# Low parts of split weights: an accumulating SBUF-to-SBUF DMA in place of a GpSimd subtraction, in the first two mixers

## The chip, the core and the metric

One core of a Trainium2 chip runs the whole program. Its engines run their own instruction streams in order: TensorE (PE; its weight loads are listed apart as PEld), VectorE (DVE), ScalarE (ACT), GpSimd (POOL) and SyncE (SP), which here only issues DMAs. The metric is the device time of one execution in microseconds.

## The reference

The reference is a stack of ten phases on a sequence of 512 tokens with 1024 features, all in float32. The first block has two layers; each is a mixer and a feed-forward block. The second block has two layers of a mixer, cross attention to 256 memory tokens, and a feed-forward block. The change touches the mixers of the first block:

```
h    = rmsnorm(x, g)
proj = h @ w_in          # 1024 x 4896: qa ka va | qd kd vd | beta, decay | z | two gates
y_attn = attention(rope(rmsnorm(qa)), rope(rmsnorm(ka)), va) @ w_o_attn
q, k, v = silu(depthwise_conv_5(qd | kd | vd)); q, k = l2norm(q), l2norm(k)
o    = gated_delta(q, k, v, beta, g) + flip(gated_delta(flipped))   # 8 chunks of 64 tokens, 8 heads
y_dn = rmsnorm(o) * silu(z) @ w_o_dn
x    = x + (sigmoid(gate0) * y_attn + sigmoid(gate1) * y_dn) @ w_out
```

In the gated delta rule each chunk needs the inverse of a unit triangular 64x64 matrix for each head and direction, and then a scan over the chunks.

## The kernel before

**Split products.** A float32 product is made of three matmuls in PE's fp32r format: both the weights and the activations are split into a high part (the value rounded to fp32r) and a low part (the value less the high part). `proj` (lines 480 to 491) does for each of a projection's chunks of 128 features: high weights by high activations (L487), high weights by low activations (L490), low weights by high activations (L491), all into one PSUM bank of 128x512.

**Weights.** The weights lie in HBM packed by groups of 256 output columns: row p of a group holds, for each of kc chunks of 128 input features, 256 columns. `fetch` (L459) loads a group with one DMA from SP into a `wraw` tile of a pool of two buffers. `wload` (L464) then cuts the group into pieces of four chunks by 128 columns (128x512 numbers): ACT casts a piece into `whi` (L474), and POOL subtracts, `wlo = wraw - whi` (L475 through the helper `tt`, L383). Both `whi` and `wlo` have four buffers, so a group of 8 chunks fills them once; a piece's cast waits until PE has used the piece four places before. The value weights of the cross attention are cut by pairs of chunks with all 256 columns (`rows=True`).

**A mixer** (`_mix`, L642) has 19 groups of `win` (`in_win`), one narrow group `wbd` of 32 columns, eight groups of 128 columns each of `woa` and `wod`, and four groups of `wout`. Its work is written as generators that are merged by hand with estimated costs: first the convolutions (`conv_tile`, L688 to L698: ACT scales, DVE adds four shifted taps at L697) and the norms (`l2`, with `rsqrt` L385 to L398 on small tiles); then `inside` (L820), which builds the chunk matrices with ACT, DVE and POOL (L843 to L853) and stores them to scratch tensors in HBM (`dnscr`, `scrK`, `scrN`, `scrT`), beside the projections of v and z; then `solve` (L1012), DVE's 30 steps of the triangular inverse on the tile N (loaded from `scrN` and `scrT`), beside the attention's projections; then the attention's core (L933), and the scan (L1180 to L1250) beside the `woa` projection; then the `wod` projection, the output projection `wout`, and the next phase's norm. The Tile framework allocates the buffers, places the semaphores, and orders each engine's stream by its own planner's costs, in the order of emission where nothing speaks against it.

SP's queue carries all weight fetches and all scratch stores and loads in one order. POOL's queue holds the subtracts, and in `inside` three to four 128x512 tensor operations for each pair of heads and direction.

Of the kernel before, what the change touches and what calls it, by code (L numbers as in the profile page):

```python
# [11 lines left out]
F32 = mybir.dt.float32  # L12
F32R = mybir.dt.float32r
I32 = mybir.dt.int32
AF = mybir.ActivationFunctionType
ALU = mybir.AluOpType
# [4 lines left out]
P = 128  # L21
S = 512
D = 1024
# [21 lines left out]
def _pack_cols(w, kc, cg):  # L45

    w = np.asarray(w)
    L, K, N = w.shape
    g = N // cg
    a = w.reshape(L, kc, P, g, cg).transpose(0, 3, 2, 1, 4)  # L50
    return np.ascontiguousarray(a).reshape(L, g, P, kc * cg)


def _cols(v):
# [115 lines left out]
EV_HEADS = ((1, 0), (0, 0), (1, 1), (0, 1), (1, 2), (0, 2), (0, 3), (1, 3))  # L170
# [35 lines left out]
def host_arrays(inputs):  # L206
    g = lambda k: np.asarray(inputs[k])
    A = {}
    A["x"] = np.ascontiguousarray(g("x")[0].T).reshape(8, P, S)
    A["mem"] = _pack_cols(np.asarray(g("mem_2")).transpose(0, 2, 1), 8, NMEM)[0, 0]  # L210
    A["vec"] = _vec_layout(inputs)[1]
    A["cst"] = CST_ARR
    A["rope"] = np.ascontiguousarray(_rope_tables())
    A["rett"] = _ret_tables()
    A["hgm"] = _hg_masks()
    A["dsat"] = _dsa_tables()
    A["relb"] = np.concatenate([g("rel_bias_2"), np.ones((1, 8), np.float32)], axis=0)
    w = g("w_in")
    qa, ka, va = w[..., :512], w[..., 512:640], w[..., 640:768]
    qd, kd, vd = w[..., 768:1280], w[..., 1280:1792], w[..., 1792:2304]  # L220
    bd, z, gate = w[..., 2304:2336], w[..., 2336:2848], w[..., 2848:]

    by_head = lambda a: a.reshape(2, -1, 2, 2, 2, 64).transpose(0, 1, 2, 4, 3, 5).reshape(2, -1, 512)
    z = by_head(z)
    qa = qa.reshape(2, D, 4, P)[..., PERM_A].reshape(2, D, 512)
    ka = ka[..., PERM_A]
    A["win"] = _pack_cols(np.concatenate([kd, qd, vd, qa, ka, va, z, gate], axis=-1), 8, 256)
    A["wbd"] = _pack_cols(bd, 8, 32)
    A["woa"] = _pack_cols(g("w_o_attn"), 4, 128)
    A["wod"] = _pack_cols(by_head(g("w_o_dn").transpose(0, 2, 1)).transpose(0, 2, 1), 4, 128)  # L230
    A["wout"] = _pack_cols(g("w_out"), 8, 256)
    A["wup"] = _pack_cols(g("w_up"), 8, 256)
    for nm, key in (("wdn", "w_down"), ("fdn", "ffn_w_out_2")):
        w = g(key)
        A[nm] = np.concatenate([_pack_cols(w[:, :1024], 8, 256), _pack_cols(w[:, 1024:2048], 8, 256)], axis=1)
        A[nm + "c"] = _pack_cols(w[:, 2048:], 6, 256)

    ev, eo = g("ev_w_in_2").reshape(1, D, 8, 4, P), g("ev_w_out_2").reshape(1, 2, 4, P, D)
    ev = [ev[:, :, 5]] + [ev[:, :, (slice(0, 4), [4, 6, 7])[i == 0], h] for i, h in EV_HEADS]
    A["evin"] = _pack_cols(np.concatenate(ev, axis=2).reshape(1, D, 4096), 8, 256)  # L240
    A["evout"] = _pack_cols(np.concatenate([eo[:, 1 - i, h] for i, h in EV_HEADS], axis=1), 8, 256)

    od = g("od_w_in_2").reshape(1, D, 3, 8, P).transpose(0, 1, 3, 2, 4).reshape(1, D, 3072)
    A["odin"] = _pack_cols(od, 8, 256)
    A["odout"] = _pack_cols(g("od_w_out_2"), 8, 256)
    A["xaq"] = _pack_cols(g("xa_w_q_2"), 8, 256)
    A["xakv"] = _pack_cols(g("xa_w_kv_2"), 8, 256)
    A["xao"] = _pack_cols(g("xa_w_o_2"), 8, 256)
    A["fup"] = _pack_cols(g("ffn_w_in_2"), 8, 256)
    return A  # L250


# [53 lines left out]
class Prog:  # L306
    def __init__(self, ctx, tc, A, out, first):
        self.ctx, self.tc, self.nc, self.A, self.out = ctx, tc, tc.nc, A, out
        nc = self.nc
        pool = lambda name, bufs=1, **kw: ctx.enter_context(tc.tile_pool(name=name, bufs=bufs, **kw))  # L310
        self.cp = pool("cp")
        self.xp = pool("xp")
        self.wr = pool("wr", 2)
        self.whl = pool("whl", 4)
        self.actp = pool("actp", 8)
        self.nrm = pool("nrm")
        self.psb_ = pool("psb", 2, space=PSUM)
        self.dr = pool("dr", 1, space=DRAM)
        self.ph = None

        self.vect = self.cp.tile([P, NVEC], F32, name="vect")
        self.cst = self.cp.tile([P, NCST], F32, name="cstt")
        self.x = [self.xt() for m in range(8)]
        self.xsrc = A["x"]
        nc.scalar.dma_start(out=self.vect, in_=A["vec"])
        nc.scalar.dma_start(out=self.cst, in_=A["cst"])

        self.first = []
        for m in range(8):
            nc.sync.dma_start(out=self.x[m], in_=A["x"][m])  # L330
            if m == 1:
                self.first = [self.fetch(s, 8, n) for s, n in first]
        self.ident = self.c("ident")
        self.ones = self.c("ones")
# [121 lines left out]
        return ps  # L456


    def fetch(self, src, kc, cg):  # L459
        raw = self.wr.tile([P, kc, cg], F32, name="wraw", tag="wraw")  # L460
        self.nc.sync.dma_start(out=raw, in_=src.rearrange("p (k c) -> p k c", k=kc))
        return raw

    def wload(self, src, kc, cg, rows=False):  # L464


        nc = self.nc
        raw = self.first.pop(0) if self.first else self.fetch(src, kc, cg)
        step, width = (2, cg) if rows else (4, min(P, cg))

        def piece(k, o):
            part = raw[:, k:min(k + step, kc), o:o + width]
            hi, lo = (self.whl.tile(list(part.shape), F32R, name=n, tag=n) for n in ("whi", "wlo"))
            nc.scalar.copy(hi, part)  # L474
            self.tt(lo, part, hi.bitcast(F32), ALU.subtract, "gpsimd")  # L475
            return k, hi, lo

        return [[piece(k, o) for k in range(0, kc, step)] for o in range(0, cg, width)]

    def proj(self, ps, w, acts, n=S, behind=None):  # L480

# [48 lines left out]
    def out_proj(self, wsrc, acts, nxt, k0=0, scale=None, final=True, behind=None):  # L530
        nc = self.nc
        kc = len(acts)
        for g in range(4):
            ws = self.wload(wsrc[g][:, k0 * 256:(k0 + kc) * 256], kc, 256)
            for j in range(2):
                m = 2 * g + j
                ps = self.psb()
                self.proj(ps, ws[j], acts, behind=behind)
                if scale is None:
                    self.tt(self.x[m], ps, self.x[m], ALU.add)  # L540
                else:
                    nc.vector.scalar_tensor_tensor(self.x[m], ps, scale, self.x[m], ALU.mult, ALU.add)
                if final:
                    self.x_done(m, nxt)
# [92 lines left out]

    def mix(self, l, nm, nxt):
        with self.phase("mix") as mp:
            self._mix(l, nm, nxt, mp)  # L640

    def _mix(self, l, nm, nxt, mp):  # L642
        nc, tc = self.nc, self.tc
# [976 lines left out]
    def _cross(self, l, nm, nxt, xp):  # L1620
        nc, gs = self.nc, self.gs
        wkv, wq = self.A["xakv"][l], self.A["xaq"][l]
# [26 lines left out]
        for k in range(8):  # L1649
            a = gs("mact", 8, (P, 2, M), F32R)  # L1650
            g = self.vec(f"xm{l}", k)
            hi = nc.scalar.activation(a[:, 0], mem[:, k], AF.Copy, scale=g)
            lo = nc.vector.scalar_tensor_tensor(a[:, 1], mem[:, k], g, a[:, 0].bitcast(F32), ALU.mult, ALU.subtract)
# [18 lines left out]
        for h in range(4):  # L1672
            ws = self.wload(wkv[h], 8, 256)
# [9 lines left out]
            for x in ks:  # L1683
                self.tt(x, x, ps, ALU.mult)
                kn.append(gs("kn", 4, (P, 2, M), F32R))
                self.split(kn[-1], x)
            ws = self.wload(wkv[4 + h], 8, 256, rows=True)
            vt = [gs("vt", 4, (P, 2, M), F32R) for _ in range(2)]
            pv = [self.psb() for _ in range(2)]
            for t in range(2):  # L1690
                tok = slice(t * P, (t + 1) * P)
                o = pv[t][:, :M]
                for k, hi, lo in ws[0]:
                    for i in range(2):
                        nc.tensor.matmul(o, ma[k + i][:, 0, tok], hi[:, i], start=k + i == 0, stop=False)
                        nc.tensor.matmul(o, ma[k + i][:, 0, tok], lo[:, i], start=False, stop=False)
                        nc.tensor.matmul(o, ma[k + i][:, 1, tok], hi[:, i], start=False, stop=k + i == 7)
                v = gs("kx", 3, (P, M))
                nc.scalar.activation(v, o, AF.Copy, scale=mr.rc[:, t])
                self.split(vt[t], v, "gpsimd")  # L1700
# [3 lines left out]
            for q2 in range(2):  # L1704
                ps = self.psf()
                for t in range(2):
                    tk, o = slice((2 * q2 + t) * P, (2 * q2 + t) * P + P), ps[:, t * M:t * M + M]
                    for i in range(2):
                        a, b = qs[i], kn[i]
# [9 lines left out]
                for t in range(2):  # L1719
                    p = pr[:, t * M:t * M + M]  # L1720
# [3 lines left out]
                for t in range(2):  # L1724
                    p = pr[:, t * M:t * M + M]
# [64 lines left out]
```

## Time and profile before

| | |
|---|---|
| median of three timed runs | 3455.85 us (3452.78 to 3457.21) |
| profiled execution | 3445.89 us |
| span from its first to its last instruction | 3444.1 us |
| mean granted TensorE clock | 0.979 of 2.4 GHz |
| busy: PE, PEld, DVE, ACT, POOL | 94%, 77%, 59%, 43%, 52% |
| first mixer, by its weight fetches and last matmuls | about 0 to 538 us |
| second mixer | about 886 to 1422 us |

The profiled execution and the timed runs are different executions; a sum made from the profile stands against 3445.89 us. Busy shares over the whole span mix phases that are bound by PE with phases that are not, so the stretches have to be looked at one by one.

### The profile page before, as it was taken

What the parts mean: (1) busy time and instruction counts of PE and PEld (TensorE: products, weight loads), DVE (VectorE), ACT (ScalarE), POOL (GpSimd) and SP (SyncE); (2) the same over time, 40 slices, a digit from 0 to 9 for tenths busy, and PEclk for the clock granted to TensorE, in tenths of its full rate; (3) what the DMA queues carried; (4) which work ended last, traced back from release to release, by engine and by line L of the source; (5) the groups of instructions that cost most, each with busy time, mean ns of one, the idle gap of its engine ahead of it and who ended that gap; (6) DMA issues with size and microseconds to landing.
All of it is one profiled execution on the core that took longest, in us unless ns stands there. A gap on an engine that the chain in (4) does not pass through costs nothing. (4 is left out here: it accounts for less than half of the span.)

```text
span 3444.1 us, 46891 instructions
## 1 busy us (share of the span) xinstructions
PE 3227.7 (94%) x17342; PEld 2655.6 (77%) x17342; DVE 2030.8 (59%) x3571; ACT 1483.2 (43%) x2766; POOL 1806.1 (52%) x1493
## 2 busy tenths in 40 slices
PE   8888899999987889999999898999999998999999
PEld 6666778888766667788877776878888887888887
DVE  8988555554698866464466676553223786653222
ACT  4526534343553553443353325443334444544332
POOL 4653365444565434654456556565556335555554
PEclk9999999999998999999999998999999999999999
DMA  4532542222354234222232113223223212222222
GB/s 148 160 89 62 119 127 98 98 89 92 121 158 124 73 81 133 100 99 92 98 112 86 62 47 103 85 99 121 94 98 107 78 67 101 88 87 98 98 97 87
DMA packets 135869, 342.53 MB, mean 99 GB/s; under 512 B 43056, under 2 KB 80304, under 8 KB 106969
## 3 DMA queue, kind: packets, MB, share of 16 engines
q1 hardware_dynamic: 134208, 336.04, 30.5%
q10 hardware_dynamic: 1432, 3.49, 0.4%
q8 instruction: 138, 2.26, 0.3%
q14 instruction: 91, 0.74, 0.1%
HBM read 312.15 MB, written 29.97 MB: 99 GB/s over the span
## 5 line engine op out<-in xcount | busy, mean ns | idle before, releaser
L383 POOL TENSOR_TENSOR wlo<-wraw,whi 128x512 fp32r<-128x512 f32 (+2 forms) x1044 | 1369.1, 1316 | 1397.9 <-ACT whi L474 1359.6
L474 ACT CAST whi<-wraw 128x512 fp32r<-128x512 f32 (+2 forms) x1044 | 631.5, 608 | 1129.5 <-PE psb L490 835.2
L487 PE MATMUL psb<-act,whi 128*128 128x512 f32 x1888 | 758.8, 402 | 59.6 <-DVE x L383 19.6
L491 PE MATMUL psb<-act,wlo 128*128 128x512 f32 x1888 | 751.5, 399 | 3.2 <-POOL wlo L383 3.0
L490 PE MATMUL psb<-act,whi 128*128 128x512 f32 x1888 | 752.6, 399 | 0.8 <-DVE act L277 0.6
L487 PEld LDWEIGHTS psb<-act,whi 128*128 128x128 f32 x1888 | 363.5, 193 | 140.0 <-issue 43.4
L491 PEld LDWEIGHTS psb<-act,wlo 128*128 128x128 f32 x1888 | 362.2, 192 | 81.1 <-POOL wlo L383 5.6
L490 PEld LDWEIGHTS psb<-act,whi 128*128 128x128 f32 x1888 | 363.4, 192 | 75.0 <-DVE act L277 2.3
L383 DVE TENSOR_TENSOR x<-psb,x 128x512 f32<-128x512 f32 x168 | 115.2, 689 | 377.0 <-PE psb L491 376.6
L487 PE MATMUL ps<-act,whi 128*128 128x512 f32 (+1 forms) x720 | 280.7, 390 | 3.4 <-ACT rB L303 3.4
L491 PE MATMUL ps<-act,wlo 128*128 128x512 f32 (+1 forms) x720 | 280.2, 389 | 0.0
L490 PE MATMUL ps<-act,whi 128*128 128x512 f32 (+1 forms) x720 | 280.2, 389 | 0.0
L487 PE MATMUL psb<-mid,whi 128*128 128x512 f32 x704 | 276.7, 394 | 1.0 <-DVE x L383 1.0
L491 PE MATMUL psb<-mid,wlo 128*128 128x512 f32 x704 | 276.2, 392 | 0.0
L490 PE MATMUL psb<-mid,whi 128*128 128x512 f32 x704 | 273.6, 389 | 0.0
L487 PEld LDWEIGHTS ps<-act,whi 128*128 128x128 f32 (+1 forms) x720 | 133.9, 186 | 33.7 <-ACT rB L303 4.6
L491 PEld LDWEIGHTS ps<-act,wlo 128*128 128x128 f32 (+1 forms) x720 | 133.9, 186 | 29.4
L490 PEld LDWEIGHTS ps<-act,whi 128*128 128x128 f32 (+1 forms) x720 | 133.9, 186 | 29.1
L491 PEld LDWEIGHTS psb<-mid,wlo 128*128 128x128 f32 x704 | 132.1, 188 | 30.5
L487 PEld LDWEIGHTS psb<-mid,whi 128*128 128x128 f32 x704 | 132.3, 188 | 29.3 <-DVE x L383 1.5
L490 PEld LDWEIGHTS psb<-mid,whi 128*128 128x128 f32 x704 | 132.1, 188 | 29.5
L383 DVE TENSOR_TENSOR cv<-ps,cv 128x512 f32<-128x512 f32 (+1 forms) x60 | 41.5, 692 | 175.9 <-PE ps L491 106.5
(437 smaller groups left out, 5712.3 us busy)
## 6 DMA issues: line engine op xcount, KB each, us to landing
wraw<-in_wup SPq DMA_DIRECT2D x44, 1024.0 KB, 4.8
wraw<-in_fup SPq DMA_DIRECT2D x44, 1024.0 KB, 4.8
wraw<-in_win SPq DMA_DIRECT2D x38, 1024.0 KB, 5.0
wraw<-in_wdn SPq DMA_DIRECT2D x16, 1024.0 KB, 4.8
wraw<-in_evin SPq DMA_DIRECT2D x16, 1024.0 KB, 4.8
wraw<-in_xakv SPq DMA_DIRECT2D x16, 1024.0 KB, 4.9
wraw<-in_fdn SPq DMA_DIRECT2D x16, 1024.0 KB, 4.8
wraw<-in_odin SPq DMA_DIRECT2D x12, 1024.0 KB, 4.9
```

The costliest lines, as they stand in the source:

```text
L383: getattr(self.nc, eng).tensor_tensor(out, a, b, op)
L474: nc.scalar.copy(hi, part)
L487: mm = nc.tensor.matmul(ps, hi[:, i], acts[k][:, 0, :n], start=k == 0, stop=False)
L490: nc.tensor.matmul(ps, hi[:, i], acts[k][:, 1, :n], start=False, stop=False)
L491: nc.tensor.matmul(ps, lo[:, i], acts[k][:, 0, :n], start=False, stop=k == kc - 1)
```

## The change

In the two first mixers a piece's low part is made in another way. ACT casts the high part as before; ACT then writes the negative of the high part into `wlo`; and a DMA from POOL's queue adds the piece of `wraw` to it, SBUF to SBUF (`accum_op=ALU.add`). In all other phases POOL subtracts as before. For all groups of 256 columns the packing in HBM becomes two halves of 128 columns, each with its chunks behind one another, so that a piece is one run of 2 KB in each row of `wraw`; `out_proj` now names the chunks that it wants (`k0`, `n`) in place of a slice. The value weights of the cross attention keep the old packing (`wrows`).

```diff
+def _pack_tiles(w, kc):
+    a = _pack_cols(w, kc, 256)
+    L, g = a.shape[:2]
+    return np.ascontiguousarray(a.reshape(L, g, P, kc, 2, P).transpose(0, 1, 2, 4, 3, 5)).reshape(L, g, P, kc * 256)
...
-    A["win"] = _pack_cols(np.concatenate([kd, qd, vd, qa, ka, va, z, gate], axis=-1), 8, 256)
+    A["win"] = _pack_tiles(np.concatenate([kd, qd, vd, qa, ka, va, z, gate], axis=-1), 8)
...
-    def fetch(self, src, kc, cg):
-        raw = self.wr.tile([P, kc, cg], F32, name="wraw", tag="wraw")
-        self.nc.sync.dma_start(out=raw, in_=src.rearrange("p (k c) -> p k c", k=kc))
-        return raw
+    def fetch(self, src, kc, cg, k0=0, n=None):
+        n, w = n or kc, min(P, cg)
+        raw = self.wr.tile([P, cg // w, n, w], F32, name="wraw", tag="wraw")
+        self.nc.sync.dma_start(out=raw, in_=src.rearrange("p (j k c) -> p j k c", k=kc, c=w)[:, :, k0:k0 + n])
+        return raw
+
+    def parts(self, part):
+        nc = self.nc
+        hi, lo = (self.whl.tile(list(part.shape), F32R, name=n, tag=n) for n in ("whi", "wlo"))
+        nc.scalar.copy(hi, part)
+        if self.lo_dma:
+            nc.scalar.activation(lo, hi.bitcast(F32), AF.Copy, scale=-1.0)
+            nc.gpsimd.dma_start(out=lo, in_=part, accum_op=ALU.add)
+        else:
+            self.tt(lo, part, hi.bitcast(F32), ALU.subtract, "gpsimd")
+        return hi, lo
+
+    def wload(self, src, kc, cg=256, k0=0, n=None):
+        raw = self.first.pop(0) if self.first else self.fetch(src, kc, cg, k0, n)
+        n = raw.shape[2]
+        return [[(k, *self.parts(raw[:, j, k:min(k + 4, n)])) for k in range(0, n, 4)] for j in range(raw.shape[1])]
...
-            ws = self.wload(wsrc[g][:, k0 * 256:(k0 + kc) * 256], kc, 256)
+            ws = self.wload(wsrc[g], wsrc[g].shape[-1] // 256, k0=k0, n=kc)
...
     def mix(self, l, nm, nxt):
         with self.phase("mix") as mp:
+            self.lo_dma = True
             self._mix(l, nm, nxt, mp)
+            self.lo_dma = False
```

## Rows read from the trace of the kernel before

**Rows 1.** The page, part 1: busy us, share of the span, instructions.
```profile
PE 3227.7 (94%) x17342; PEld 2655.6 (77%) x17342; DVE 2030.8 (59%) x3571; ACT 1483.2 (43%) x2766; POOL 1806.1 (52%) x1493
```

**Rows 2.** Stretches: length, each engine's busy us (instructions), clock, DMA share, GB/s.
```profile
560.00:900.00 340.00, 339.68 (x1493) 280.01 (x1492) 179.58 (x200) 136.93 (x226) 172.31 (x133) 1.00 0.28 98
...
45.00:220.00 175.00, 146.61 (x718) 119.61 (x717) 154.77 (x223) 85.42 (x161) 96.90 (x67) 0.92 0.51 139
...
sum 495.00, PE 409.42 PEld 331.03 DVE 439.83 ACT 241.14 POOL 262.08; mean PE 102.36 PEld 82.76 DVE 109.96 ACT 60.28 POOL 65.52
```

**Rows 3.** Timeline from 80 us: start, us, engine, line, operation, names, count.
```profile
80.61 0.18 DVE L383 TENSOR_TENSOR rsq<-rc 128x32 f32<-128x32 f32 x1
...
81.27 0.60 ACT L474 CAST whi<-wraw 128x512 fp32r<-128x512 f32 x1
81.31 0.68 DVE L383 TENSOR_TENSOR x<-x,cstt 128x512 f32<-128x512 f32 x1
...
81.95 2.99 POOL L383 TENSOR_TENSOR wlo<-wraw,whi 128x512 fp32r<-128x512 f32 x2 [2.52 <-ACT whi L474]
82.02 1.78 DVE L697 SCALAR_TENSOR_TENSOR kq<-pad,vect,kq 128x512 f32<-128x512 f32 x1
...
84.92 0.74 DVE L697 SCALAR_TENSOR_TENSOR kq<-pad,vect,kq 128x512 f32<-128x512 f32 x1
```

**Rows 4.** DVE's groups by form, 45 to 220 us: busy, mean ns, idle before.
```profile
L697 DVE SCALAR_TENSOR_TENSOR kq<-pad,vect,kq 128x512 f32<-128x512 f32 x22 | 21.0, 954 | 2.0 <-ACT kq L695 1.8
L697 DVE SCALAR_TENSOR_TENSOR cv<-pad,vect,cv 128x512 f32<-128x512 f32 x16 | 16.6, 1041 | 1.0 <-ACT cv L695 0.8
...
L383 DVE TENSOR_TENSOR x<-x,kkqq 128x512 f32<-128x512 f32 x8 | 12.3, 1556 | 0.0
...
L397 DVE SCALAR_TENSOR_TENSOR rsq<-rsq 128x32 f32<-128x32 f32 x6 | 3.1, 509 | 0.1
```

**Rows 5.** Waits: DVE's of 45 to 220, PE's of 45 to 300: us, times, longest.
```profile
DVE x L383 <- PE psb L491: 6.0, 1, 6.0
DVE ntmp L383 <- DMA N<-scrT: 5.9, 1, 5.9
DVE kq L697 <- ACT kq L695: 1.8, 3, 0.9
...
PE psb L487 <- DVE x L383: 9.7, 4, 3.8
...
PE psb L491 <- POOL wlo L383: 1.1, 1, 1.1
```

**Rows 6.** The stretches of rows 2, instructions that touch wlo: PE, PEld, POOL.
```profile
45.00:220.00 175.00, 65.81 (x161) 32.12 (x161) 55.93 (x38) 0.92 0.51 139
...
sum 495.00, PE 165.64 PEld 80.92 POOL 148.17; mean PE 41.41 PEld 20.23 POOL 37.04
```

**Rows 7.** DMA issues of 256 KB: queue, count, KB each, median us to landing.
```profile
dnscr<-s SPq DMA_DIRECT2D x32, 256.0 KB, 3.4
...
ti<-N SPq DMA_DIRECT2D x16, 256.0 KB, 5.1
...
xsp<-x SPq DMA_DIRECT2D x8, 256.0 KB, 2.0
```

**Rows 8.** Timeline of SP around the wod weights.
```profile
479.52 0.33 SPq L461 DMA_DIRECT2D wraw<-in_wod  x1
...
482.46 0.33 SPq L461 DMA_DIRECT2D wraw<-in_wout  x1
...
485.40 0.33 SPq L461 DMA_DIRECT2D wraw<-in_wout  x1
```

**Rows 9.** Timeline of PE, the first and the last of nine matmuls.
```profile
21.01 0.40 PE L487 MATMUL psb<-act,whi 128*128 128x512 f32 x1
...
22.88 0.39 PE L491 MATMUL psb<-act,wlo 128*128 128x512 f32 x1
```

**Rows 10.** Timeline of ACT in the same place, with its idle time.
```profile
482.66 0.62 ACT L474 CAST whi<-wraw 128x512 fp32r<-128x512 f32 x1 [1.26 <-DMA wraw<-in_wod]
```

More of the change, by code (lines that the diff above doesn't have):

```diff
@@ L230, in host_arrays @@
     A["wod"] = _pack_cols(by_head(g("w_o_dn").transpose(0, 2, 1)).transpose(0, 2, 1), 4, 128)
-    A["wout"] = _pack_cols(g("w_out"), 8, 256)
-    A["wup"] = _pack_cols(g("w_up"), 8, 256)
+    A["wout"] = _pack_tiles(g("w_out"), 8)
+    A["wup"] = _pack_tiles(g("w_up"), 8)
     for nm, key in (("wdn", "w_down"), ("fdn", "ffn_w_out_2")):
         w = g(key)
-        A[nm] = np.concatenate([_pack_cols(w[:, :1024], 8, 256), _pack_cols(w[:, 1024:2048], 8, 256)], axis=1)
-        A[nm + "c"] = _pack_cols(w[:, 2048:], 6, 256)
+        A[nm] = np.concatenate([_pack_tiles(w[:, :1024], 8), _pack_tiles(w[:, 1024:2048], 8)], axis=1)
+        A[nm + "c"] = _pack_tiles(w[:, 2048:], 6)
     ev, eo = g("ev_w_in_2").reshape(1, D, 8, 4, P), g("ev_w_out_2").reshape(1, 2, 4, P, D)
     ev = [ev[:, :, 5]] + [ev[:, :, (slice(0, 4), [4, 6, 7])[i == 0], h] for i, h in EV_HEADS]
-    A["evin"] = _pack_cols(np.concatenate(ev, axis=2).reshape(1, D, 4096), 8, 256)
-    A["evout"] = _pack_cols(np.concatenate([eo[:, 1 - i, h] for i, h in EV_HEADS], axis=1), 8, 256)
+    A["evin"] = _pack_tiles(np.concatenate(ev, axis=2).reshape(1, D, 4096), 8)
+    A["evout"] = _pack_tiles(np.concatenate([eo[:, 1 - i, h] for i, h in EV_HEADS], axis=1), 8)
     od = g("od_w_in_2").reshape(1, D, 3, 8, P).transpose(0, 1, 3, 2, 4).reshape(1, D, 3072)
[L244 to L249, printed above, removed]
+    A["odin"] = _pack_tiles(od, 8)
+    A["odout"] = _pack_tiles(g("od_w_out_2"), 8)
+    A["xaq"] = _pack_tiles(g("xa_w_q_2"), 8)
+    w = g("xa_w_kv_2")
+    A["xakv"] = np.concatenate([_pack_tiles(w[..., :1024], 8), _pack_cols(w[..., 1024:], 8, 256)], axis=1)
+    A["xao"] = _pack_tiles(g("xa_w_o_2"), 8)
+    A["fup"] = _pack_tiles(g("ffn_w_in_2"), 8)
     return A
@@ L456, in spread, with wrows @@
         return ps
-    def fetch(self, src, kc, cg):
-        raw = self.wr.tile([P, kc, cg], F32, name="wraw", tag="wraw")
-        self.nc.sync.dma_start(out=raw, in_=src.rearrange("p (k c) -> p k c", k=kc))
-        return raw
[L464 to L478, printed above, removed]
+    def fetch(self, src, kc, cg, k0=0, n=None):
[17 more added lines that the diff above has]
+        return [[(k, *self.parts(raw[:, j, k:min(k + 4, n)])) for k in range(0, n, 4)] for j in range(raw.shape[1])]
+    def wrows(self, src, kc):
+        raw = self.wr.tile([P, kc, 256], F32, name="wraw", tag="wraw")
+        self.nc.sync.dma_start(out=raw, in_=src.rearrange("p (k c) -> p k c", k=kc))
+        return [(k, *self.parts(raw[:, k:k + 2])) for k in range(0, kc, 2)]
     def proj(self, ps, w, acts, n=S, behind=None):
@@ L639, in mix @@
         with self.phase("mix") as mp:
+            self.lo_dma = True
             self._mix(l, nm, nxt, mp)
+            self.lo_dma = False
     def _mix(self, l, nm, nxt, mp):
@@ L1686, in _cross @@
                 self.split(kn[-1], x)
-            ws = self.wload(wkv[4 + h], 8, 256, rows=True)
+            ws = self.wrows(wkv[4 + h], 8)
             vt = [gs("vt", 4, (P, 2, M), F32R) for _ in range(2)]
@@ L1692, in _cross @@
                 o = pv[t][:, :M]
-                for k, hi, lo in ws[0]:
+                for k, hi, lo in ws:
                     for i in range(2):
```

## The prediction, made before the change was run

> **What bounds the kernel now.** I read the page's busy line first: TensorE (PE) is busy 94% of the span, so at most 6% can be won anywhere [rows 1]. Then busy time by stretch, to see where PE's idle time is. In the first feed-forward block PE has no gap at all: 339.7 of 340 us; a change there can only lose. In the two mixers it is different. The four stretches 45 to 300 us and 960 to 1200 us are 495 us long, and there VectorE (DVE) is the fullest engine with 439.8 us (89%), PE has 409.4 (83%), ScalarE (ACT) 241.1 and GpSimd (POOL) 262.1 [rows 2]. The 86 us that PE lacks there are most of what the mixers can give back.
>
> Next the timeline, for why DVE is full. A multiply-add of line 697 on 128x512 takes 0.74 us when POOL is quiet; the one that starts at 82.02, while POOL runs two weight subtracts, takes 1.78. A 128x512 tensor-tensor with two SBUF operands takes 0.68, a 128x32 step 0.18 [rows 3]. The groups of DVE's instructions by form tell how often this happens: the means lie far above those free durations [rows 4]. DVE's instructions with two operands in SBUF are stretched while POOL works.
>
> Last the waits, for who waits on whom. In 45 to 220 us DVE's idle time ends with PE once (6.0 us) and with the load of N once (5.9); the longest total on ACT is 1.8. PE for its part waits mostly for DVE to empty its banks (9.7 in one group), and only 1.1 us, once, for a low part [rows 5]. So in these stretches the order of cause is POOL, then DVE, then PE.
>
> **The change, part by part.** By the code a mixer has 19 column groups of four pieces, two pieces of wbd, eight each of woa and wod, and four groups of wout: 76 + 2 + 16 + 16 = 110 pieces, 220 in both. A piece is 128x512 numbers of whi and of wlo.
>
> *POOL's subtract is removed.* In 45 to 220 us it is 55.9 of POOL's 96.9 us, in the four stretches 148.2 of 262.1 [rows 2, 6]. What DVE gets back: from the groups, 22 x (954 - 740) ns = 4.7 us, 16 x (1041 - 740) = 4.8, 8 x (1556 - 680) = 7.0, and 6 x (509 - 180) = 2.0 for line 397, whose two companions in the same chain I count alike, 5.9 in all [rows 3, 4]. That is 22.4 us seen in a few groups. Bounds: below, only the subtract's share of POOL's time, 58%, gives 13; above, each subtract costs DVE its own length, 55.9. I take 25, near what is seen, since smaller groups add and POOL's other work takes away: 0.45 us of DVE per us of subtract. Over the four stretches that is 0.45 x 148.2 = 66 us, and DVE falls from 440 to 374, under PE's 409. PE becomes the fullest. Now the fullest engine reaches 89%; if PE then reaches 90%, the 495 us become 454: **41 us gained**. Bounds: 0 where dependences hold the stretch, 64 at 95% (431 us). I take 41, since it only asks that PE be served as well as DVE is now. The stretches outside are PE's already and I give them nothing.
>
> *ACT's negative is added.* It is a pass like the cast, 0.60 us [rows 3]: 220 x 0.60 = 132 us, of which 100 pieces, 60 us, fall in the four stretches; ACT goes to 301 of 454 us, 66%. Behind it wait ACT's tanh, copies and scalings, and DVE behind those. As DVE hardly waits for ACT there [rows 5], it is mostly covered by ACT's idle time; **5 us**, bounds 0 and 60.
>
> *The accumulating DMA is added.* The trace has no DMA that is issued from POOL and none that adds. Its 256 KB land 2.0 to 5.1 us after the issue in plain transfers [rows 7]. I take 4.5 from the end of the negative to the landing, near the slow end, since it reads two sources and shares the engines. The issue itself costs POOL at least SP's 0.33 us [rows 8] and, by the nearest POOL row, about what the subtract cost (1.5 us each, [rows 3]); between these POOL is no fuller than now, so nothing is charged. The Trainium skill prices it lower: its page "DMA: Bandwidth & Descriptors", section "Anatomy of one DMA — SWDGE (gpsimd) path", gives about 2.0 us plus bytes over 436 GB/s, 2.6 us for a piece as an estimate; the lateness below would shrink to some 4 us and the profile to about 3416 us.
>
> *How late is the low part?* whi and wlo have four buffers. Nine matmuls start in 2.1 us, 0.234 us apart [rows 9], so a piece of twelve lasts PE 2.8 us and a freed buffer is wanted again 8.4 us later. Now cast and subtract take 0.6 + 1.5 of it; then 0.6 + 0.6 + 4.5 = 5.7. That leaves 2.7 us, so in a steady row nothing waits. It fails in three places. (1) At the start there is no lead: 0.6 + 4.5 - 1.5 = 3.6 us later, **3 us** charged once. (2) wod: its pieces come one by one through the two raw buffers, and a buffer's next fetch waits until the low part has been made. SP issues these fetches 2.94 us apart now [rows 8], and ACT already waits for their data [rows 10]. The cycle grows by 3.6 us for two buffers, 1.8 a piece; for the four of eight that aren't fetched beforehand 7.2, less 2.7 of lead, about 5 a mixer, **10 us**. (3) Scattered places with a short lead, such as the one wait above [rows 5]: **4 us** for both. SP's own queue stands behind the raw buffer too (the stores of dnscr, scrN and scrT); with the 5.9 us wait for N in view I charge **2 us**.
>
> *The packing by 128 columns* moves no work: the fetches bring the same bytes in one piece. Only the half fetches of three later output projections become two runs per row; they are issued a group ahead and PE works meanwhile, so nothing; with that cover gone an SP issue of 0.33 us [rows 8] more for each of some three dozen, 12 us.
>
> Sum: 41 - 5 - 3 - 10 - 4 - 2 = **17 us less**. The profiled execution took 3445.9 us (span 3444.1 and 1.8 around it), so 3429 in its own terms. The median of the three timed runs lies 10 us above that execution, so I forecast **3439 us**. 0.2%, 7 us, is about what can be told from no change.
>
> **The rivals.**
>
> *The low part lands too late (slower).* The place is the ring of four. Cast, negative, landing L, PE's 2.8 and about 0.9 of ACT's queue make 4.9 + L against 11.3 us for four pieces; so from L = 6.4 us on, the DMA paces PE. At L = 7 the cycle is 11.9, 0.15 us a piece; over the half of the 220 that PE paces 17 us; wod 2 x 12 (four pieces by 3.05 us, without lead), the start 6, the rest 11: 58 against 41, and the time is 3473. For it: DMA engines are half busy in 45 to 220 us [rows 2], and a 256 KB store of N takes 5.1 [rows 7]. Against: the other rows of this size are at 2.0 and 3.4 us. The Trainium skill names something that would lengthen L: in "SBUF — State Buffer", "SBUF: two separate sides", DVE passes in a two-port mode keep POOL from writing the descriptors. No row here shows it.
>
> *POOL's issue holds DVE as the subtract did.* Then the change does not do what it says: no 66 us, and the costs remain, 3480 at worst, 3459 with half the relief. For it: POOL still works for every piece. Against: nothing large is read by POOL any more. The Trainium skill ("SBUF — State Buffer", "Who interferes with whom") sides against it: a DVE instruction with two SBUF inputs contends with POOL instructions that read SBUF, and not with one that only writes. No run here has shown that yet.
>
> *The relief is real but goes nowhere.* DVE's free time turns into waits for ACT, for N's load or for the scratch stores, and half of the 41 us is kept: 20 - 24, so 3456 to 3460, no change. For it: N's load ends a DVE wait in each mixer [rows 5]. Against: DVE has under 12% idle time.
>
> **How the numbers follow.** Forecast 0.55, late landing 0.20, held by the issue 0.10, goes nowhere 0.15. The forecast's own range is 3402 (64 gained, 10 spent) to 3452. The range for 8 in 10 reaches up to the late landing and the half-held case, **3402 to 3480**. Faster takes the forecast and a third of "goes nowhere": 0.60; same, most of the rest of it: 0.13; slower, late landing and most of the held case: 0.27.
>
> **What the profile would show.** Right: in 45 to 300 and 960 to 1200 us line 697's mean falls from about 1 us towards 0.74, POOL's busy time loses about half, DVE falls below PE and both mixers shorten by some 10 us each; PE's waits for wlo appear around wod. The feed-forward blocks stay as they are. Wrong by size: landings beyond 6 us with PE waiting for wlo in steady rows, or line 697 still at 1 us. Wrong in kind: a different order of the instructions on DVE or ACT, which the planner's own costs for the new instructions may bring about and no row of before can tell.

## The result

The changed kernel takes 3507.92 us (median of four runs, 3503.59 to 3514.57), the kernel before, run beside it, 3455.2. The ratio is 1.0155, with a 95% interval of 1.0137 to 1.0172: 53 us slower. The forecast was 3439 with a range to 3480, so the sign is wrong and the time lies outside the range.

The profiled execution took 3503.59 us with a span of 3501.8. First the page's busy line, with the lines of two DMA queues (packets, MB, share of 16 engines' span):

```profile
PE 3249.5 (93%) x17342; PEld 2669.5 (76%) x17342; DVE 1913.7 (55%) x3571; ACT 1608.4 (46%) x2986; POOL 1680.0 (48%) x1493
...
q1 hardware_dynamic: 138816, 336.04, 30.3%
q0 software_dynamic: 31680, 56.90, 9.5%
```

DVE fell by 117 us against [rows 1], ACT rose by 125, POOL fell by 126, and there is a new queue, q0, of the accumulating DMAs. The stretch of [rows 2] in the first mixer, in the same columns:

```profile
45.00:220.00 175.00, 146.53 (x717) 118.84 (x716) 129.41 (x232) 109.31 (x203) 72.73 (x69) 0.92 0.87 204
220.00:300.00 80.00, 72.81 (x375) 58.76 (x374) 64.51 (x128) 53.59 (x101) 28.81 (x27) 1.00 0.58 119
```

The first row shows one half of the case; the other half lies around wod, further below. DVE's busy time falls by 25.4 us of 175 (154.8 to 129.4). PE does not get one of them (146.6 to 146.5); it gets some in the next 80 us. The DMA engines' share rose from 0.51 to 0.87. The relief itself is where it was looked for; the groups of DVE's instructions by form, same stretch (answering to [rows 4]):

```profile
L721 DVE SCALAR_TENSOR_TENSOR kq<-pad,vect,kq 128x512 f32<-128x512 f32 x24 | 17.9, 745 | 3.0 <-ACT kq L719 2.7
L721 DVE SCALAR_TENSOR_TENSOR cv<-pad,vect,cv 128x512 f32<-128x512 f32 x16 | 17.3, 1082 | 3.4 <-ACT cv L719 3.3
...
L393 DVE TENSOR_TENSOR x<-x,kkqq 128x512 f32<-128x512 f32 x8 | 6.6, 819 | 1.5 <-POOL x L393 1.5
```

Line 697 is line 721 now; its means for kq went from 954 to 745 ns, the undisturbed 0.74 us of [rows 3]. The product x went from 1556 to 819. The taps of cv (the shifted adds of the convolution) did not gain (1041 to 1082): some of them stand beside POOL's tensor operations of `inside`, which are not changed. One such pair:

```profile
89.24 4.30 POOL L393 TENSOR_TENSOR s<-kq,eg 128x512 f32<-128x512 f32 x2
90.61 1.78 DVE L721 SCALAR_TENSOR_TENSOR cv<-pad,vect,cv 128x512 f32<-128x512 f32 x1
```

In this stretch the five taps that meet such an operation take 1026 to 2574 ns; of all others none takes more than 755. What became of the 25 us is in DVE's waits of the same stretch, where [rows 5] had 6.0, 5.9 and 1.8:

```profile
DVE ntmp L393 <- DMA N<-scrT: 12.8, 1, 12.8
DVE sums L426 <- PE ps L422: 10.1, 1, 10.1
DVE x L393 <- POOL x L393: 5.3, 4, 2.1
DVE s L867 <- DMA dnscr<-s: 5.1, 2, 3.0
```

33.3 us in these four. DVE starts on N at 188.95 us before and at 190.10 now: it reaches N sooner and N is not there sooner. In the second mixer the wait for N went from 5.6 to 11.5 us. The landings in 45 to 300 us (count, size, median us from issue to landing), then N's load before:

```profile
wlo<-wraw POOLq DMA_DIRECT2D x56, 256.0 KB, 5.4
wraw<-in_win SPq DMA_DIRECT2D x14, 1024.0 KB, 6.2
...
ti<-N SPq DMA_DIRECT2D x8, 256.0 KB, 6.9
...
N<-scrT SPq DMA_DIRECT2D x1, 1024.0 KB, 17.8
```
```profile
N<-scrT SPq DMA_DIRECT2D x1, 1024.0 KB, 13.7
```

N's load from scratch takes 17.8 us where it took 13.7. The store of N took 5.1 in [rows 7] and takes 6.9 now. PE's waits, first of the whole span, then of 45 to 300 us, where [rows 5] had 1.1 us for a low part:

```profile
PE psb L513 <- DMA wlo<-wraw: 54.7, 33, 5.6
```
```profile
PE ps L542 <- DVE cv L393: 9.6, 1, 9.6
PE psb L513 <- DMA wlo<-wraw: 7.7, 6, 2.5
```

In the first mixer such waits come to 27.2 us: 6.0 in the first 45 us, 7.7 in the stretch where the rows are dense, and 13.6 from 300 us on. SP's timeline of the first mixer's end (start, duration, count) shows where:

```profile
458.03 25.23 SPq L473 DMA_DIRECT2D wraw<-in_wod  x6
...
488.88 0.33 SPq L473 DMA_DIRECT2D wraw<-in_wod  x1
...
491.21 0.33 SPq L473 DMA_DIRECT2D wraw<-in_wod  x1
...
499.67 0.33 SPq L473 DMA_DIRECT2D wraw<-in_wout  x1
...
540.50 0.33 SPq L473 DMA_DIRECT2D wraw<-in_wup  x1
```

Taking such first fetches of a weight as marks, each stage's length before and after, in us:

```
stage, from first fetch to first fetch   first mixer        second mixer
win (from wbd) to woa                    368.3 -> 363.3     367.7 -> 375.6
woa to wod                                86.1 ->  93.1      85.8 ->  91.4
wod to wout                               26.4 ->  41.6      26.4 ->  42.1
wout to wup                               35.2 ->  40.8      35.2 ->  40.0
```

The first mixer loses 22.8 us, the second 33.9; wod and wout hold 41.3 of the 56.7. Behind each mixer some 3 us come back before the next mark, and the first cross attention loses 8.4 (from the first fetch of mem to that of xao 125.1 us before, 133.5 after). Its code is as before, but its instructions stand in another order on the engines; why the planner orders it so was not tried. It does not take the DMAs: the two kernels below in which the mixers make no low part at all take 131.9 and 135.3 us there. By the same marks six of the runs below take 125 to 128 us there and eleven take 131 to 138, so up to 13 us of a run's difference can come from this place and not from the stage that was changed.

### The profile page after: what moved, and what is told of

Its sections match the earlier page's. It is cut to its first block, busy times and chain, and to the rows that moved or that the text cites. A ratio compares the mean times of both kernels' runs of the same rounds, so it can differ in the third digit from the quotient of the medians.

```text
span 3501.8 us, 47341 instructions
## 1 busy us (share of the span) xinstructions
PE 3249.5 (93%) x17342; PEld 2669.5 (76%) x17342; DVE 1913.7 (55%) x3571; ACT 1608.4 (46%) x2986; POOL 1680.0 (48%) x1493
## 3 DMA queue, kind: packets, MB, share of 16 engines
q1 hardware_dynamic: 138816, 336.04, 30.3%
q0 software_dynamic: 31680, 56.90, 9.5%
## 5 line engine op out<-in xcount | busy, mean ns | idle before, releaser
L393 POOL TENSOR_TENSOR wlo<-wraw,whi 128x512 fp32r<-128x512 f32 (+1 forms) x824 | 1062.1, 1293 | 1061.1 <-ACT whi L481 1031.1
L484 POOL DMA_DIRECT2D wlo<-wraw x220 | 194.2, 919 | 419.5 <-ACT wlo L483 392.2
L513 PEld LDWEIGHTS psb<-mid,wlo 128*128 128x128 f32 x704 | 132.2, 188 | 30.3
```

The costliest lines, as they stand in the source:

```text
L393: getattr(self.nc, eng).tensor_tensor(out, a, b, op)
L484: nc.gpsimd.dma_start(out=lo, in_=part, accum_op=ALU.add)
L513: nc.tensor.matmul(ps, lo[:, i], acts[k][:, 0, :n], start=False, stop=k == kc - 1)
```

## The experiments

In the expectations A is the DMA as the cause, B ACT's second pass, C the packing and the order of work that comes with it. A1 puts the DMA's price in the cycle of the raw buffers around wod. All ratios are against the kernel before, run beside it on the same chip. Differences between two versions are taken from their medians, and stages from the profiled executions.

**1. The change taken apart.**

The packing alone, no piece by DMA:

```diff
-            self.lo_dma = True
```


> The new packing alone; POOL subtracts everywhere. Theory A (the loss comes from the DMAs: they land late on short rings and crowd the 16 DMA engines) and theory B (it comes from the 132 us of negatives on ACT) both expect 3450 to 3470 us, at most the 7 us that the later phases lost. Theory C (packing, or the other order that it brings) expects most of the 53 us: 3490 to 3510.

Measured: 3455.04 us, ratio 0.9998 (0.9987 to 1.0009). C falls: the packing costs and brings nothing.

The cast and the negative, but no DMA behind them:

```diff
-            nc.gpsimd.dma_start(out=lo, in_=part, accum_op=ALU.add)
```


> The change with the DMA left out: wlo holds only the negative of whi, so the low parts in the two mixers are not computed. A: the DVE relief stays, the lateness and the traffic go: 3400 to 3445 us, faster than before. B: the negatives stay, so the time stays above before: 3480 or more.

Measured: 3397.53 us, ratio 0.9836 (0.9821 to 0.9851). Without the DMA the change is 58 us faster than before, with it 53 slower: the DMA costs 110 us. By the marks of the table above the stages take 334.4, 88.2, 25.2 and 36.1 us in the first mixer and 332.2, 92.5, 25.2 and 36.1 in the second. Set against these, the changed kernel loses 72 us in win, 4 in woa, 33 from wod to wout and 9 from wout to wup; the rest of the span gives some 9 back. The stretch of [rows 2] in this kernel:

```profile
45.00:220.00 175.00, 158.40 (x780) 130.75 (x780) 148.45 (x265) 119.43 (x225) 49.87 (x35) 0.97 0.52 147
```

PE does 158.4 us where it did 146.6: when no low part has to be waited for, PE is served as forecast (90% of 175 is 157.5), and the DMA share stays at 0.52. The 495 us of [rows 2] hold 1980 of PE's matmuls in the kernel before. Counted from the start, the same matmuls take less time here (43.2 to 268.2 and 929.9 to 1136.7 us) and in the changed kernel (48.6 to 292.4 and 991.0 to 1223.3 us); the lines have the sums, this kernel first:

```profile
sum 431.80, PE 389.86 PEld 321.03 DVE 364.47 ACT 296.25 POOL 110.99; mean PE 194.93 PEld 160.52 DVE 182.23 ACT 148.12 POOL 55.50
```
```profile
sum 476.10, PE 403.42 PEld 325.96 DVE 359.05 ACT 297.92 POOL 195.25; mean PE 201.71 PEld 162.98 DVE 179.53 ACT 148.96 POOL 97.63
```

For this work 63 us are gained without the DMA and 19 with it.

Neither negative nor DMA; the high part is used for the low one:

```diff
-            nc.scalar.activation(lo, hi.bitcast(F32), AF.Copy, scale=-1.0)
-            nc.gpsimd.dma_start(out=lo, in_=part, accum_op=ALU.add)
-        else:
+            return hi, hi
...
```


> The change with neither negative nor DMA in the two mixers: the third matmul takes whi in place of wlo, so no low part is made there. This shows the whole worth of taking the subtract from POOL. A and B: 3390 to 3430 us. B also expects it to be more than 40 us faster than the kernel that keeps the negatives; A at most 15. If the relief goes nowhere: 3450 to 3460.

Measured: 3390.92 us, ratio 0.9817 (0.9802 to 0.9832). The negative costs 6.6 us of 3397.5.

The negative, and GpSimd adds instead of the DMA:

```diff
-            nc.gpsimd.dma_start(out=lo, in_=part, accum_op=ALU.add)
+            self.tt(lo, part, lo.bitcast(F32), ALU.add, "gpsimd")
```


> ACT's negative with a POOL addition in place of the DMA: POOL works as before, ACT has 220 passes more. This prices the negative alone. A: 3455 to 3475 us. B: 3490 or more.

Measured: 3455.27 us, ratio 1.0001 (0.9992 to 1.0011). B falls. And POOL's tensor operation, not the way the low part is computed, is what holds DVE: with it back all of the gain is gone. The stretch of [rows 2], and DVE's taps of kq in it:

```profile
45.00:220.00 175.00, 150.70 (x729) 122.58 (x728) 156.78 (x223) 109.11 (x203) 97.11 (x68) 0.93 0.51 139
```
```profile
L721 DVE SCALAR_TENSOR_TENSOR kq<-pad,vect,kq 128x512 f32<-128x512 f32 x22 | 20.8, 944 | 1.6 <-ACT kq L719 1.4
```

**2. What in the DMA costs.**

GpSimd's subtract for wbd, woa and wod, the DMA for the other 184 pieces:

```diff
+        self.lo_dma = dma and cg == 256
```


> The change, but POOL subtracts for woa, wod and wbd, whose pieces come one by one through the two raw buffers; the DMA makes the other 184 low parts. Between its first fetch of wod and of wout the change takes 41.7 and 42.0 us, before took 26.4 and 26.3. Theory A1 (the raw buffer's cycle through the DMA holds wod) expects 3470 to 3485 us. Theory A2 (all of the loss is the traffic beside the scratch stores and the load of N) expects 3500 to 3510, no change.

Measured: 3453.46 us, ratio 0.9992 (0.9979 to 1.0006). 54 us come back for 36 of 220 pieces, more than A1 asked for (its range began at 3470); from wod's first fetch to wout's it is 26.4 us again in both mixers. A2 falls as the whole cause.

All by DMA, but woa and wod are fetched four column groups at a time:

```diff
+                if m % 4 == 0:
+                    raw = self.wr.tile([P, 4, 4, P], F32, name="wraw", tag="wraw")
+                    nc.sync.dma_start(out=raw, in_=wo[m:m + 4].rearrange("m p (k c) -> p m k c", c=P))
...
-                self.proj(ps, self.wload(wo[m], 4, P)[0], ys, ...)
+                self.proj(ps, [(0, *self.parts(raw[:, m % 4]))], ys, ...)
```


> The change, with woa and wod fetched four column groups at a time into one raw buffer, so that a buffer's cycle spans four pieces; every low part still by DMA. A1: 3470 to 3490 us, and PE no longer waits on whi and wlo in wod. A2: no change, 3500 to 3510.

Measured: 3475.38 us, ratio 1.0065 (1.0048 to 1.0082): 32.5 us of the loss go without a single DMA fewer on POOL, as A1 had it. PE's waits for low parts are 45.0 us, not 54.7. From wbd's first fetch to wup's the mixers take 530.4 and 538.0 us where the changed kernel has 538.8 and 549.0; 5 us more come from the first cross attention. The edit makes one fetch of four, so the raw buffers' cycle and the number of fetches change together here.

Plain DMAs in the accumulating ones' place, two for each piece, whose data nobody waits for:

```diff
-            nc.gpsimd.dma_start(out=lo, in_=part, accum_op=ALU.add)
+            if part.shape[2] == P:
+                for i in range(2):
+                    scr = self.dr.tile([P, S], F32, name="spare", tag="spare", bufs=12)
+                    nc.gpsimd.dma_start(out=scr, in_=self.vect[:, :S])
```


> The kernel with the negative alone (3397.5 us), and in place of each accumulating DMA two plain DMAs of 256 KB from POOL's queue that nobody waits for, from a constant tile to scratch in HBM. The low parts are not computed. It has about the traffic, without the wait. A2 expects 3420 us or more, a longer load of N and longer landings of the fetches; if only the wait for the low part counts (A1 and the ring of four): 3397 to 3410.

Measured: 3516.68 us, ratio 1.0179 (1.0154 to 1.0204). The low parts are not made in it. It is no clean match: as no low part holds these DMAs back, all 432 of them run in the first mixer, the last at 543 us. The stretch of [rows 2] and one of the second mixer:

```profile
45.00:220.00 175.00, 149.91 (x735) 120.46 (x735) 118.42 (x214) 108.39 (x199) 107.44 (x163) 0.91 0.98 334
1000.00:1175.00 175.00, 162.72 (x822) 132.48 (x821) 143.14 (x248) 120.46 (x222) 43.81 (x31) 0.98 0.54 152
```

woa's first fetch comes at 423.4 us where the kernel without any such DMA has 336.1; in the second mixer, with a share of 0.54, nothing is lost. So load on the DMA engines alone, with no low part to wait for, can cost a mixer 87 us, but at 334 GB/s, which the changed kernel's 204 does not reach. POOL issues four times as often there as in the changed kernel, too, so the 87 is not all load.

The DMA kept, but for 32 of 512 columns of a piece, 16 KB:

```diff
-            nc.gpsimd.dma_start(out=lo, in_=part, accum_op=ALU.add)
+            nc.gpsimd.dma_start(out=lo[:, 0, :32], in_=part[:, 0, :32], accum_op=ALU.add)
```


> The change with accumulating DMAs of 128x32 numbers (16 KB) in place of 256 KB: the wait for a landing stays, nearly all bytes go. Most of each low part is not computed. If bytes count (A2): 3400 to 3430 us. If the fixed time of a DMA from POOL counts (A1, rings): 3460 or more.

Measured: 3436.66 us, ratio 0.9953 (0.9937 to 0.9969), between the two forecasts. With the bytes gone 71 us go (3507.9 to 3436.7); what a DMA costs whatever its size is the other 39 (3436.7 to 3397.5). By the marks win takes 343.5 and 350.8 us and wod 30.6 and 30.2: 45 of the 72 us of win go with the bytes, and 23 of the 33 of wod. The stretch and the landing in 45 to 300 us:

```profile
45.00:220.00 175.00, 157.12 (x776) 128.55 (x774) 148.57 (x257) 114.14 (x211) 86.79 (x79) 0.95 0.61 149
```
```profile
wlo<-wraw POOLq DMA_DIRECT2D x60, 16.0 KB, 2.9
```

PE has 157 us again although POOL issues just as many DMAs, so POOL's issuing does not hold DVE.

**3. One stage alone by DMA.** Each of these has a tuple of the win groups that go by DMA, GpSimd subtracts the rest, and `wload` takes the choice as an argument:

```diff
+LO = (0, 1, 2, 3)
...
-            ws = self.wload(win[g], 8, 256)
+            ws = self.wload(win[g], 8, 256, dma=g in LO)
```

q and k of the delta rule, groups 0 to 3:

> Low parts by DMA only for the first four column groups of win (q and k of the delta rule, 32 of 220 pieces, before inside); GpSimd subtracts all others. Theory T (a 256 KB accumulating DMA harms where it meets inside's scratch stores and loads; elsewhere DVE's relief is kept): DVE is fullest here, so 8 to 20 us less than before, 3434 to 3446. Theory E (every such DMA costs about what its relief gives, wherever it stands): within 4 us of before, 3450 to 3458.

Measured: 3459.9 us, ratio 1.0024 (1.0014 to 1.0034), about 8 us more. Neither theory has that.

v and z, groups 4, 5, 9, 10, beside `inside`:

> Low parts by DMA only for the four groups of v and z (32 of 220 pieces), which are projected beside inside, where the chunk matrices go to scratch tensors and come back. Theory T: the wait for N's load is 10 us or more and the time is 5 to 25 us above before, 3459 to 3479. Theory E: within 4 us of before, 3450 to 3458, and N's wait as before, about 6 us.

Measured: 3440.92 us, ratio 0.9966 (0.9952 to 0.9979), about 12 less; N's wait is 4.8 us. T's claim on the place is wrong, and E falls too.

The attention's groups and the gates, 6 to 8 and 11 to 18:

> Low parts by DMA only for the eleven groups of the attention's q, k, v and of the two gates (88 of 220 pieces), beside solve, the attention's core and the scan. Theory T: 5 to 20 us less than before, 3434 to 3449, as the scratch traffic is over or small there. Theory E: within 6 us of before.

Measured: 3444.98 us, ratio 0.9983 (0.9972 to 0.9994), about 6 less, which both theories allow.

All of win but v and z:

> Low parts by DMA for all groups of win but v's and z's (120 of 220 pieces); wbd, woa, wod and wout are subtracted on GpSimd. Theory T: the gains of the two runs above add up, 15 to 35 us less than before, 3419 to 3439, faster than both kernels. Theory E: within 8 us of before.

Measured: 3454.7 us, ratio 1.0005 (0.9993 to 1.0017). No gain, and T falls with its gains. E holds; the parts of the two runs (+8 and -6) also add up to this, though 6 us of this run lie in the first cross attention (131.2 us).

woa and wod alone:

```diff
-                self.proj(ps, self.wload(wo[m], 4, P)[0], ys, ...)
+                self.proj(ps, self.wload(wo[m], 4, P, dma=True)[0], ys, ...)
```


> Low parts by DMA only for woa and wod (64 of 220 pieces); GpSimd subtracts all others. Theory W (woa and wod lose by themselves, through the cycle of the raw buffers, as their groups come one by one): the stretch from wod's first fetch to wout's first is 40 us or more in both mixers where it was 26, and the time is 30 to 60 us above before, 3484 to 3514. Theory L (they lose because all the other DMAs load the engines): wod's stretch under 32 us and the time at most 15 us above before.

Measured: 3495.95 us, ratio 1.0119 (1.0104 to 1.0134): 41 us, with 32 pieces in both mixers by DMA (the 64 above is a miscount). The mixers take 22.5 and 16.9 us more from wbd's first fetch to wup's; the first cross attention takes 12.8 more, which is not these pieces' doing. W holds: wod's stage grows to its 40 us, nearly so in the second mixer. SP's timeline, and the landings in 455 to 500 us:

```profile
468.64 25.61 SPq L476 DMA_DIRECT2D wraw<-in_wod  x6
...
508.80 0.33 SPq L476 DMA_DIRECT2D wraw<-in_wout  x1
...
540.21 0.33 SPq L476 DMA_DIRECT2D wraw<-in_wup  x1
```
```profile
wlo<-wraw POOLq DMA_DIRECT2D x9, 256.0 KB, 3.6
wraw<-in_wod SPq DMA_DIRECT2D x7, 256.0 KB, 2.7
```

The DMA engines are not full here (a share of 0.50 in 455 to 500 us), both DMAs land as soon as anywhere, and still wod takes 40.2 us (37.9 in the second mixer). The waits tell what holds a fetch (455 to 505 us), and what ACT then lacks (455 to 500 us):

```profile
SPq L476 <- DMA wlo<-wraw: 37.7, 9, 10.6
```
```profile
ACT whi L484 <- DMA wraw<-in_wod: 17.0, 5, 6.4
```

A raw buffer is taken for 2.7 (fetch) + 0.6 (cast) + 0.6 (negative) + 3.6 (from POOL's issue to the landing) = 7.5 us, and half a us between these steps: SP fetches at 468.64 us and into the same buffer again at 476.66, 8.0 us later. Two buffers give a piece each 4.0 us at best, where PE needs 2.8. Measured are 5.0 (40.2 for eight pieces), as the steps also wait for ACT and for POOL's other work.

wout alone:

```diff
+            ws = self.wload(wsrc[g], ..., dma=scale is not None)
```


> Low parts by DMA only for wout (32 of 220 pieces). If the parts add up, the run with all but wbd, woa and wod by DMA (1 us under before) less the three win runs (-10 us together) leaves 9 us for wout: 3460 to 3466, with PE waiting for wlo in wout's rows. If they do not add up, within 4 us of before.

Measured: 3461.07 us, ratio 1.0027 (1.0017 to 1.0037): 9 us, the sum that the parts had. But it is not all wout's: from wout's first fetch to wup's the mixers take 3.9 and 6.6 us more, the first cross attention 8.7 more, and the rest gives some back. The waits of PE for low parts that were expected are not there: 1.5 us in the whole run.

v, z, attention and gates:

> Low parts by DMA for v, z, the attention's groups and the gates (120 of 220 pieces), GpSimd's subtract for q and k of the delta rule, wbd, woa, wod and wout. If the parts add up, 18 us less than before, 3432 to 3440, the fastest of the whole versions. If the DMAs of one part hold those of the other, 0 to 10 us less.

Measured: 3426.43 us, ratio 0.9922 (0.9908 to 0.9937). 27 us faster than before and 81 faster than the change: the fastest of the versions that leave nothing out. It is more than the 18 that the parts add up to; why was not tried.

Two runs for the loss of q and k: groups 1 and 3 alone (`LO = (1, 3)`), and these added to the fastest.

> Low parts by DMA only for the third and fourth of the four q and k groups (16 of 220 pieces); the first two, with which a mixer begins, are subtracted on GpSimd. Theory S (q and k lost 8 us because PE has no lead at the mixer's start): PE's first 45 us are as busy as before, 32 of 45, and the time is 3 to 10 us under before. Rival (these pieces lose wherever they stand): 2 to 8 us above before.

Measured: 3444.16 us, ratio 0.9973 (0.9961 to 0.9984), 9 less: S holds. (Groups 1 and 3 are the third and fourth that a mixer takes.) The first 45 us with groups 0 to 3, and with 1 and 3 only; below them PE's largest wait for a low part in the first:

```profile
0.00:45.00 45.00, 27.06 (x111) 19.27 (x111) 23.63 (x44) 24.05 (x41) 15.70 (x24) 1.00 0.69 196
```
```profile
0.00:45.00 45.00, 31.27 (x118) 21.12 (x119) 30.20 (x45) 20.79 (x35) 21.84 (x25) 0.96 0.49 176
```
```profile
PE psb L517 <- DMA wlo<-wraw: 7.9, 2, 7.3
```

PE loses some 4 to 5 us at the start of the first mixer when its first pieces go by DMA (32.4 us busy before).

> The fastest mix so far (v, z, attention and gates by DMA, 0.9922 of before) plus the third and fourth group of q and k: 136 of 220 pieces. Theory S: 0.987 to 0.992 of before, 3410 to 3425. Rival: 0.993 to 0.996.

Measured: 3438.99 us, ratio 0.9958 (0.9941 to 0.9974). The rival's side: 16 pieces that gain 9 us by themselves lose 13 here. The stretch of [rows 2] in the fastest version, then with the 16 pieces added; then, from DVE's timelines, its first step on N and its first step on the attention's tile th in each:

```profile
45.00:220.00 175.00, 152.10 (x751) 122.81 (x750) 145.79 (x244) 108.34 (x202) 82.88 (x74) 0.96 0.81 192
```
```profile
45.00:220.00 175.00, 145.84 (x714) 118.46 (x713) 124.53 (x229) 106.91 (x200) 69.67 (x66) 0.91 0.84 193
```
```profile
175.94 0.68 DVE L396 TENSOR_TENSOR th<-th,ps 128x512 f32<-128x512 f32 x1
...
185.90 0.22 DVE L396 TENSOR_TENSOR ntmp<-N 128x60 f32<-128x60 f32 x1 [3.20 <-DMA N<-scrT]
```
```profile
193.56 0.22 DVE L396 TENSOR_TENSOR ntmp<-N 128x60 f32<-128x60 f32 x1 [16.29 <-DMA N<-scrT]
...
200.51 0.68 DVE L396 TENSOR_TENSOR th<-th,ps 128x512 f32<-128x512 f32 x1
```

Nearly the same load on the DMA engines (0.81 and 0.84), 21 us less of DVE, 13 us more of waiting for N. Of these 13, 7.7 are N landing later (at 193.6 and not 185.9 us). The other 5.4 are the order: in the fastest version DVE does steps of the attention before it turns to N, and with the 16 pieces added they stand behind N. So the load is not the only suspect; the planner's order is a rival that no run here separates from it. The whole change has the same picture as the slower of the two (0.87, 129.4 and 12.8).

## Why the prediction was wrong

**What bounds the kernel: right.** POOL's subtract holds DVE, and DVE holds PE. The run with the negatives and no DMA shows it, the run with GpSimd's add shows the opposite. This also settles the rival that POOL's issue holds DVE: with as many issues and 16 KB each, PE is served (157 of 175 us). In the changed kernel the taps of line 721 in 45 to 220 us take at most 755 ns where they meet an issue alone, and 745 in the mean for kq. The Trainium skill ("SBUF — State Buffer", "Who interferes with whom") has a DVE instruction with two SBUF inputs contend with POOL instructions that read SBUF and not with one that only writes; by that rule line 721 should run free beside POOL's issues, and the trace agrees, with that 745 ns.

**DVE's relief: right in size; its worth was too small.** 25 us were taken for 45 to 220 us, 25.4 are seen, with nine instructions more in the stretch. With the DMA out of the way the 495 us shrink by 63 us where 41 were forecast. PE's share there is the 90% that was taken (389.9 of 431.8 us), but its own work, taken as fixed at 409 us, is 390. The granted clock, a mean over stretches at 2.4 and at 1.2 GHz, is 0.97 and 0.98 there, where before, with PE busy 83% of the time, had 0.93 and 0.94. That 3455.05 less 3390.92 is 64, the term's upper bound, is luck: the bound stood for PE at 95%.

**ACT's negative: right.** 5 charged, 6.6 measured.

**The DMA: the step that failed.** Charged were 3 + 10 + 4 + 2 = 19 us; it costs 110. The prediction asked of the DMA only when its own data land, found that "in a steady row nothing waits", and left 2 us for all that its transfers do to others. In its place the runs showed 72 us lost in win and 33 around wod, against the kernel with the negatives alone. By term:

- *SP's queue and N's load, 2 us.* This is the largest miss. Of the 63 us that the relief brings in the dense stretches, 44 are lost. N's wait went from 5.9 to 12.8 us, and the stores to scratch got slower with it (ti, 5.1 to 6.9). The prediction had the share of the engines in view (0.51) and did not add the new transfers to it: 0.87. With 16 KB in place of 256, 45 of the 72 us of win come back, and PE's own waits for low parts (7.7 us in the first mixer's dense stretch, 8.8 in the second's) are too short to explain that; this points to what the bytes do to other transfers. How much of it goes through N, through the other stores and loads, or through the other order of work, no run here separates.
- *wod, 10 us.* The mechanism was right, two raw buffers held until the low part is made, but it was charged for four pieces of eight, less a lead of 2.7. With woa and wod alone, wod's stage is 13.8 and 11.5 us longer, and wout's gives back 3.8 in each mixer: 17.7 net for both, where 10 stood. A delay of 1.7 us a piece (13.8 / 8) is close to the 1.8 forecast; all eight pay. woa, for which nothing was charged, is 8.6 and 9.7 us longer, though not by its DMAs alone: with only q and k by DMA it is 5 and 6 us longer, too. The 2.94 us between fetches that the prediction took from [rows 8] are those of the last ones; the mean of the eight was 3.3 (26.4 / 8).
- *Scattered places, 4 us for both mixers.* By the marks wout alone is 3.9 and 6.6 us longer. Where wod's and wout's low parts both come by DMA it grows: from wod's first fetch to wup's the first mixer takes 61.6 us before, 71.6 with woa and wod alone, 65.5 with wout alone, 82.5 with all: 20.9 longer, and not 10.0 + 3.9. That is 7 us, and 6 in the second mixer, that no single stage shows.
- *The start, 3 us, charged once.* It comes in both mixers: PE's first 45 us have 32.4 us of work before and 27.1 with q and k by DMA, and in the 45 us from wbd's fetch in the second mixer it is 45.0 and 40.0, with a granted clock of 1.00 (2.4 GHz throughout) and 0.92 (part of it at 1.2). That is 10.

**"In a steady row nothing waits": nearly so.** The landing was taken as 4.5 us and is 5.4, under the 6.4 that the late landing needed; PE's waits for low parts in 45 to 300 us are 7.7. It was the others that waited. That rival had the sign right and the place wrong. "The relief goes nowhere" had the place right, N and the scratch stores, and in the dense stretches nearly the size: half of 41 us kept there, 19 measured. It had no price for wod beyond the forecast's. These two together, with the raw buffers, are what happened.

**The order of work** differs in the first cross attention, which loses 8 us, and in what DVE does before N. A new order was named as what no row of before can tell; its cause stays open.

The Trainium skill's price for a DMA on this path ("DMA: Bandwidth & Descriptors", "Anatomy of one DMA — SWDGE (gpsimd) path") made 2.6 us for a piece as an estimate; 3.6 are measured beside DMA engines at a share of 0.50 and 5.4 in the loaded stretch. They differ, and the measurement decides. The 4.5 us that the prediction took lie between these two.

## What to carry to other kernels

Work that moves from an engine to a DMA has to be charged three times: for when its data land, for the buffer that it reads and so keeps from the next fetch, and for the share of the DMA engines that it takes from every other transfer. The second is worst where pieces come one by one through two buffers: add the whole time of a buffer, divide by the buffers, and compare with what the consumer needs for a piece (8.0 / 2 against 2.8 us here). The third seems to be the dearest here, as far as the runs tell it from the order of work. And such a change is best made stage by stage: three stages lost here and two gained, and with those two alone it is 0.8% faster than before, where all of them together are 1.6% slower. A stage is best priced between marks of its own, since a part that no edit touches moved by up to 13 us.

## What the runs showed of the hardware

- An accumulating DMA took about twice the engines' time of a plain one for each MB. In the changed kernel q0 moved 56.90 MB in 9.5% of the span, 5.8 us per MB of all 16 engines (0.095 x 3501.8 / 56.90); q1 moved 336.04 MB in 30.3%, 3.2 us per MB. The plain DMAs of 256 KB that POOL issued in the traffic run took 2.7 (0.087 x 3511.0 / 113.27):

```profile
q0 software_dynamic: 34560, 113.27, 8.7%
```

- POOL's issue of an accumulating DMA took as long whatever its size: 919 ns in the mean where 216 of 220 are of 256 KB, and 924 where all are of 16 KB. A plain one of 256 KB took 545 (x432, the traffic run).

```profile
L484 POOL DMA_DIRECT2D wlo<-wraw x220 | 194.2, 919 | 419.5 <-ACT wlo L483 392.2 <-DVE S L1245 9.5 <-PE ps L1196 4.3
```
```profile
L484 POOL DMA_DIRECT2D wlo<-wraw x220 | 195.7, 924 | 377.2 <-ACT wlo L483 356.7 <-ACT whi L481 6.9 <-PE ps L983 5.2
```

- An accumulating DMA of 16 KB from POOL still landed only 2.9 us after its issue (median of 60), against 5.4 for one of 256 KB (median of 56) in the same stretch.
